# A hybrid decoder block: two of the six value jobs computed together as seven block products

## The chip, the cores and the metric

The kernel runs on one core of a Trainium2 chip. The metric is the device time in microseconds of one execution, as the median of several runs; a separate profiled execution shows where the time lies. The engines are named as in the profile: PE (TensorE, the products), DVE (VectorE), ACT (ScalarE), POOL (GpSimd) and SP (which issues most of the transfers). Each executes its own instructions strictly in the order in which the program holds them, and waits where an instruction needs what another engine has not finished.

## What is computed

One layer on 1024 tokens of 1024 features in float32: a norm, one wide projection to queries, keys, values, convolution input and two gates, dilated attention in three groups of eight heads, a causal depthwise convolution with a layer norm, the gated sum of both, an output product, and a SwiGLU feed-forward part.

```python
h = rms_norm(x, g_pre_mix[l])
z = h @ w_in[l]
q, k, v, glu_in, z_ga, z_gc = jnp.split(
    z, np.cumsum([ATTN_W, ATTN_W, ATTN_W, 2 * CONV_CHANNELS, D_MODEL]).tolist(), axis=-1)
y_attn = dilated_attention_mixer(...)            # 3 groups x 8 heads of 64
u = lax.conv_general_dilated(u, ...) + b_dw      # 31 taps, 1024 channels
u = jax.nn.silu(layer_norm(u, g_ln, b_ln))       # the convolution's norm, over channels
merged = jax.nn.sigmoid(z_ga) * y_attn + jax.nn.sigmoid(z_gc) * y_conv
x = x + rms_norm(merged @ w_mix_out[l], g_post_mix[l])
```

The values `v` are 1536 columns: six jobs of 256 columns, one for each group (three) and half of its heads (two).

## The kernel before

Every float32 operand of a product is kept as a high part, rounded by ACT, and a low part, the difference, so that a product is three products: high by high, high by low, low by high. Most of the projection is computed by a scheme with seven block products in place of eight (`winograd`, `prod`): the weights are cut into A11, A12, A21, A22 and combined to S1 to S4, the tokens into B11, B21, B22 and combined to T1 to T4 (`block_sums`, kept in `B.T`), and three accumulators X, Z, V collect the seven products. There the weights are the stationary operand and 512 columns of tokens move.

The six value jobs (`v`, L1115 on) are done the plain way: a 128 by 128 block of tokens is stationary, the weights move. For each of 8 token tiles and 8 feature tiles there is a pair of products: L1139 with 512 columns (high tokens by high and low weights) and L1140 with 256 (low tokens by high weights), 64 pairs for a job. ACT copies the result from PSUM (L1150), POOL adds its two halves (L1161), and SP stores it to `d_v`. Weight parts come from `value_weights` (ACT L207, DVE L208).

The order is written out by hand. `tick()` is called after every few products; it runs the steps that `later(n, step)` has put down for n ticks ahead, the next piece of weight preparation, and the next step of every generator in the background. In a value job a tick is four products. Beside the value jobs runs `conv_norm` (L1486 on), one such generator: it loads the eight channel blocks of the convolution, takes the mean over channels by a product on PE (L1503), subtracts it (DVE L1512), squares (ACT L1515), adds the squares up (DVE L1518), has PE sum them over partitions (L469 in `rstd`), takes one over the root on ACT and DVE (L473 to L478), spreads that over partitions by transposes on PE (L484), multiplies (DVE L1530) and applies SiLU (ACT L1533). It works on whole blocks of 128 x 1024, in steps of three or four ticks.

The attention (`attention`) is a second generator; `beat()` runs its steps between the products. Its first score waits, in the program's order, until the norm is done (`normed` reaches 9) and the first values are stored (`vn`). Before a pair's scores, `double` sets up its keys on POOL: a memset (L1078) and two copies (L1079, L1080) for each head and each half of the tokens. For the first pair the first half is queued 17 ticks after `attention` begins, the second half within its second score step. Attention needs 96 score tiles; it begins in the third value job and ends among the products of the convolution's output (`unit`, L336 to L338), where `conv_split` also prepares operands on ACT and DVE.

The last of the query and key pairs (`qk_pair`) comes right before the value jobs; on its way out DVE finishes the convolution (L868 to L881) and POOL adds its last block to the channel sum `csum` (L893).

## Time and profile before

| | us |
|---|---|
| median of 3 runs | 1675.94 |
| lowest and highest run | 1675.64, 1676.26 |
| the profiled execution | 1676.75 |
| its span on the chip | 1675.0 |
| PE busy in it | 1658.9 |

The span is what the trace covers; the profiled execution's own time is 1.75 us more. A busy PE is not a PE at its peak: a product is counted busy from its start to its end, and products overlap, so the pitch from one start to the next is the better measure of what one costs. A row of the timeline gives the start in microseconds from the span's start, the length, the engine, the line, and the tile written and read; in brackets stands the idle time of the engine before it and what ended that. A group with "x2" is several instructions in a row.

### The profile page before, as it was taken

The page shows a single profiled execution, that of the slowest core. Times are in us where ns is not written, and L with a number is a line of the kernel's source. Part 1 is how long each engine was busy: PE and PEld are TensorE (multiplying, and loading weights), DVE is VectorE, ACT ScalarE, POOL GpSimd, SP SyncE. Part 2 cuts the span into 40 slices and gives each one's busy share as a digit, 9 for nine tenths or more (in the row PEclk, how much of TensorE's full clock was granted, in tenths as well). Part 3 has the DMA queues.
Part 4 walks back from the last instruction along what each step waited for, and adds up shares of the span by engine and source line. Part 5 has one row for each costly group of instructions (what it writes and reads, how often), then busy time and mean ns, then how long its engine had stood idle before and what let it go on. Part 6 is the DMA issues. An engine that isn't in the chain of part 4 may idle for free.

```text
span 1675.0 us, 23388 instructions
## 1 busy us (share of the span) xinstructions
PE 1658.9 (99%) x8027; PEld 1384.6 (83%) x8027; DVE 1272.3 (76%) x2268; ACT 828.3 (49%) x1646; POOL 542.5 (32%) x456
## 2 busy tenths in 40 slices
PE   9999999999999999999999999999999999999998
PEld 7787888888888889988788888888888888888886
DVE  7998987789899768778876746877655566576686
ACT  7454443443444588888713357633333333354453
POOL 0038777787876366877300300000000000000000
PEclk9999999999999999999999999999999999999999
DMA  4435433455566987879998524134232223494334
GB/s 182 153 102 187 143 132 126 153 176 192 177 176 161 286 273 224 257 220 286 297 272 310 176 88 171 56 132 151 84 118 94 95 95 119 165 375 120 115 119 157
DMA packets 165178, 289.64 MB, mean 173 GB/s; under 512 B 47689, under 2 KB 79812, under 8 KB 165060
## 3 DMA queue, kind: packets, MB, share of 16 engines
q1 hardware_dynamic: 164420, 287.45, 52.5%
q8 instruction: 63, 1.03, 0.3%
q14 instruction: 55, 0.45, 0.1%
q10 hardware_dynamic: 288, 0.52, 0.1%
q0 software_dynamic: 352, 0.18, 0.1%
HBM read 197.39 MB, written 95.42 MB: 175 GB/s over the span
## 4 chain that ended last, share of the span: by engine, by line
PE 87%; issue 5%; DVE 2%; POOL 2%; ACT 2%; DMA 1%; SPq 0%; DVEq 0%; ACTq 0%; POOLq 0%
PE p L354 16%; PE p L353 16%; PE p L352 16%; PE p L2282 13%; PE p L2026 5%; PE p L1139 5%; PE p L336 2%; PE p L337 2%; PE p L338 2%; PE p L1140 2%; PE p L655 2%; PE p L1339 2%; PE p L1305 1%; PE p L1266 1%; PE p L1262 1%
## 5 line engine op out<-in xcount | busy, mean ns | idle before, releaser
L352 PE MATMUL p<-b,b 128*128 128x512 f32 x1316 | 512.7, 390 | 0.1
L354 PE MATMUL p<-b,b 128*128 128x512 f32 x1316 | 512.4, 389 | 0.2
L353 PE MATMUL p<-b,b 128*128 128x512 f32 x1316 | 512.2, 389 | 0.1
L352 PEld LDWEIGHTS p<-b,b 128*128 128x128 f32 x1316 | 247.1, 188 | 52.7 <-ACT c L411 0.5
L354 PEld LDWEIGHTS p<-b,b 128*128 128x128 f32 x1316 | 247.1, 188 | 52.5 <-POOL b L215 1.5
L353 PEld LDWEIGHTS p<-b,b 128*128 128x128 f32 x1316 | 247.1, 188 | 51.7 <-DVE b L1477 0.5
L2282 PE MATMUL p<-b,b 128*128 128x512 f32 x924 | 209.6, 389 | 0.0
L2282 PEld LDWEIGHTS p<-b,b 128*128 128x128 f32 x924 | 173.5, 188 | 36.0
L868 DVE SCALAR_TENSOR_TENSOR p<-b,par,p 128x511 f32<-128x511 f32 (+14 forms) x232 | 163.6, 738 | 0.0
L1139 PE MATMUL p<-b,b 128*128 128x512 f32 x384 | 144.2, 408 | 0.1
L214 ACT CAST b<-d 128x1024 fp32r<-128x1024 f32 x82 | 86.1, 1050 | 100.7 <-POOL d L237 56.6
L215 POOL TENSOR_TENSOR b<-d,b 128x1024 fp32r<-128x1024 f32 x43 | 104.2, 2422 | 47.6 <-ACT b L214 39.0
L1477 DVE TENSOR_TENSOR b<-b,b 128x512 fp32r<-128x512 f32 x141 | 98.9, 708 | 16.0 <-ACT b L1476 14.4
L215 DVE TENSOR_TENSOR b<-d,b 128x1024 fp32r<-128x1024 f32 x39 | 47.6, 1221 | 79.3 <-ACT b L214 79.3
L1140 PE MATMUL p<-b,b 128*128 128x256 f32 x384 | 107.7, 280 | 0.0
L1476 ACT CAST b<-b 128x512 fp32r<-128x512 f32 x141 | 86.4, 619 | 40.9 <-PE p L2282 18.5
L336 PE MATMUL p<-b,b 128*128 128x512 f32 x240 | 96.3, 401 | 0.0
L214 ACT CAST b<-b 128x1024 fp32r<-128x1024 f32 x51 | 53.6, 1052 | 85.0 <-POOL b L246 38.7
L1280 ACT ACTIVATE c<-c,stat 128x128 f32<-128x128 f32 (+1 forms) x192 | 85.2, 447 | 18.2 <-DVE stat L1270 16.9
L337 PE MATMUL p<-b,b 128*128 128x512 f32 x240 | 93.6, 390 | 0.0
L338 PE MATMUL p<-b,b 128*128 128x512 f32 x240 | 93.6, 390 | 0.0
L2026 PE MATMUL p<-b,b 128*128 128x512 f32 x384 | 89.9, 392 | 0.0
(248 smaller groups left out, 2897.0 us busy)
## 6 DMA issues: line engine op xcount, KB each, us to landing
b<-w_in SPq DMA_DIRECT2D x33, 512.0 KB, 5.8
b<-w_fi SPq DMA_DIRECT2D x29, 512.0 KB, 4.4
d<-w_in SPq DMA_DIRECT2D x25, 512.0 KB, 4.2
dk<-c SPq DMA_DIRECT2D x48, 256.0 KB, 4.3
dq<-c SPq DMA_DIRECT2D x48, 256.0 KB, 3.6
b<-dk SPq DMA_DIRECT2D x48, 256.0 KB, 6.2
d<-w_fi SPq DMA_DIRECT2D x22, 512.0 KB, 3.5
dqS<-c SPq DMA_DIRECT2D x44, 256.0 KB, 2.1
```

The source lines that it names most:

```text
L214: self.nc.scalar.copy(hi, x)
L215: self.wsplit.tensor_tensor(lo, x, f(hi), op=OP.subtract)
L336: nc.tensor.matmul(ps, hi[:, s], a, start=kt == 0, stop=False)
L337: nc.tensor.matmul(ps, hi[:, s], b, start=False, stop=False)
L352: nc.tensor.matmul(ps, hi[:, s], a, start=first and kt == 0, stop=False, skip_group_check=True)
L353: nc.tensor.matmul(ps, hi[:, s], b, start=False, stop=False, skip_group_check=True)
L354: nc.tensor.matmul(ps, lo[:, s], a, start=False, stop=kt == 3, skip_group_check=True)
L868: nc.vector.scalar_tensor_tensor(A[i][:, j:], src[i][:, :H - j], w[i], A[i][:, j:], op0=OP.mult, op1=OP.add)
L1139: nc.tensor.matmul(ps, a, w, start=kt == 0, stop=kt == KT - 1, skip_group_check=True)
L1140: nc.tensor.matmul(ps[:, 256:], b, w[:, :256], start=False, stop=kt == KT - 1, skip_group_check=True)
L2026: nc.tensor.matmul(banks[tt][nh], st, wt[:, nh * H:(nh + 1) * H], start=bool(kt == 0 and a), stop=bool(kt == KT - 1 and b))
L2282: nc.tensor.matmul(acc[t], x, y, start=first and e == 0, stop=last and e == 2, skip_group_check=True)
```

## The change

The first two value jobs, group 0 and group 1 of the first half of the heads, become one task, `quad`. It is the scheme with seven block products: rows of A are the two jobs (256 columns each), columns of A the two halves of the 1024 features, and B is the tokens' `B.T` that the earlier pairs used, which therefore stays alive a little longer. The tokens' blocks are stationary and 256 columns of weights move, high or low. `quad_prod` is one block product: 4 feature tiles by 4 token tiles by 3, 48 products, with a tick after every sixth. The sums of the weights (`quad_sum`) are made on DVE, the high parts on ACT and the low parts on POOL (`quad_split`), at ticks given by hand; those of the first block product and the loads hang on the last query and key pair (`pair`). The results go from PSUM through ACT copies and DVE additions to `d_v` in smaller stores. The other four value jobs stay as they are.

`conv_norm` now works by token halves: 16 half blocks of 128 x 512 are loaded, reduced and scaled, one step every second tick, the two halves one after the other, with a column sum on PE and a `rstd` for each half. The means are taken at tick 7, the column sums at ticks 29 and 49 of the quad's 56. While it runs beside the quad it uses the same PSUM pool.

`attention` is begun at tick 43 of the quad, and the first pair's keys are set up in four pieces 17, 19, 21 and 23 ticks later, second half included.

```diff
+        elif n < len(J) and J[n][2] == "values":
+            self.quad_first(self.quads[0], (2, 9, 3, 4, 19, 28, 29, 30))
...
-        ps = self.bank("s")
+        tag = "s" if "s" in self.tags else "g"
+        ps = self.bank(tag)
...
+    def quad_load(self, q, k):
+        x = q["r"][k] = self.slot() if k < 2 else self.ring()
+        self.nc.sync.dma_start(x, q["src"][k])
+    def quad_sum(self, q, name):
+        r, add = q["r"], self.nc.vector.tensor_tensor
+        if name == "S1":
+            q["s"] = self.ring()
+            add(q["s"], r[2], r[3], op=OP.add)
+        elif name == "S3":
+            add(r[2], r[0], r[2], op=OP.add)
+        elif name == "S2":
+            add(r[0], r[0], q["s"], op=OP.add)
+        else:
+            add(r[1], r[0], r[1], op=OP.add)
+    def quad_split(self, q, name):
+        nc, r = self.nc, q["r"]
+        k = ("A11", "A12", "S1", "A22", "S2", "S4", "S3").index(name)
+        if k == 2:
+            x, q["s"] = q["s"], None
+        else:
+            x = r[(0, 1, None, 3, 0, 1, 2)[k]]
+        hi, lo = self.slot(F32R), self.slot(F32R)
+        nc.scalar.copy(hi, x)
+        if k > 2:
+            r[(3, 0, 1, 2)[k - 3]] = None
+        nc.gpsimd.tensor_tensor(lo, x, f(hi), op=OP.subtract)
+        q["w"][name] = hi, lo
+    def quad_first(self, q, t):
+        for k, step in zip(t, [lambda: self.quad_load(q, 0), lambda: self.quad_load(q, 1), lambda: self.quad_load(q, 2),
+                               lambda: self.quad_load(q, 3), lambda: self.quad_split(q, "A11"),
+                               lambda: self.quad_sum(q, "S1"), lambda: self.quad_sum(q, "S3"),
+                               lambda: self.quad_sum(q, "S2")]):
+            self.later(k, step)
+    def quad_prod(self, ps, w, rhs, first):
+        nc = self.nc
+        hi, lo = w
+        for kt in range(4):
+            a, b = rhs[kt]
+            n = slice(kt * 256, (kt + 1) * 256)
+            for c in range(4):
+                o = ps[c // 2][:, c % 2 * 256:(c % 2 + 1) * 256]
+                t = slice(c * 128, (c + 1) * 128)
+                nc.tensor.matmul(o, a[:, t], hi[:, n], start=first and kt == 0 and c % 2 == 0, stop=False,
+                                 skip_group_check=True)
+                nc.tensor.matmul(o, a[:, t], lo[:, n], start=False, stop=False, skip_group_check=True)
+                nc.tensor.matmul(o, b[:, t], hi[:, n], start=False, stop=kt == 3 and c % 2 == 1, skip_group_check=True)
+                if c % 2:
+                    self.tick()
+    def quad(self, q, T, then):
+        nc, w = self.nc, q["w"]
+        last = then is None
...
...
+        def copy(ps, job, small=False):
+            x = result(small)
+            for b in range(2):
+                d = ordered(x[b], job[0][0])
+                if job is ja:
+                    nc.scalar.copy(d, plain(ps[b]))
+                else:
+                    nc.scalar.activation(d, plain(ps[b]), AF.Identity, scale=-1.0)
+            return x
+        def add(ps, x, job, hf):
+            for b in range(2):
+                d = ordered(x[b], job[0][0])
+                if job is ja:
+                    nc.vector.tensor_tensor(d, plain(ps[b]), d, op=OP.add)
+                else:
+                    nc.vector.tensor_tensor(d, d, plain(ps[b]), op=OP.subtract)
+            self.later(4, lambda: store(x, job, hf))
+        def two():
+            return [self.bank(), self.bank()]
+        ja, jb = q["jobs"]
+        for k, step in ((1, lambda: self.quad_split(q, "A12")), (5, lambda: self.quad_sum(q, "S4")),
+                        (9, lambda: self.quad_split(q, "S2")),
+                        (17, lambda: self.quad_split(q, "S1")), (25, lambda: self.quad_split(q, "S3")),
+                        (33, lambda: self.quad_split(q, "S4")), (41, lambda: self.quad_split(q, "A22"))):
+            self.later(k, step)
+        X, Z = two(), two()
+        self.quad_prod(X, w.pop("A11"), operands("B11"), True)
+        x1 = copy(X, ja, True)
+        self.quad_prod(Z, w.pop("A12"), operands("B21"), True)
+        add(Z, x1, ja, 0)
+        Z = x1 = None
+        self.quad_prod(X, w.pop("S2"), operands("T2"), False)
+        x2 = copy(X, ja)
+        V = two()
+        self.quad_prod(V, w.pop("S1"), operands("T1"), True)
+        v1 = copy(V, jb)
+        self.quad_prod(X, w.pop("S3"), operands("T3"), False)
+        add(X, v1, jb, 1)
+        v1 = None
+        self.quad_prod(V, w.pop("S4"), operands("B22"), False)
+        add(V, x2, ja, 1)
+        V = x2 = None
+        self.quad_prod(X, w.pop("A22"), operands("T4"), False)
+        o = result()
+        for b in range(2):
+            nc.scalar.activation(ordered(o[b], jb[0][0]), plain(X[b]), AF.Identity, scale=-1.0)
+        def end():
+            store(o, jb, 0)
+            self.vn = jb[1] + 1
+        self.later(3, end)
...
-        self.later(17, lambda p=nxt: self.double(p, 0))
+        for i in range(4):
+            self.later(17 + 2 * i, lambda p=nxt, i=i: self.double(p, i // 2, (i % 2,)))
...
-                if u == 1:
-                    self.double(cur, 1, (1,) if cur[2]["z"][1] else (0, 1))
+                if u == 1 and s:
+                    self.double(cur, 1, (1,))
...
+        add = nc.vector.tensor_tensor
+        A = {}
+        def load(hf, j):
+            x = self.slot()
+            for e in range(2):
+                b = 2 * j + e
+                nc.sync.dma_start(x[:, e * H:(e + 1) * H], self.d_conv[b][:, hf * H:(hf + 1) * H])
+                A[hf, b] = x[:, e * H:(e + 1) * H]
+        def average(hf):
+            ps = self.bank()
+            nc.tensor.matmul(ps, self.mean_col.to_broadcast([128, 128]), self.csum[:, hf * H:(hf + 1) * H],
+                             start=True, stop=True)
+            m = self.half()
+            nc.scalar.copy(m, ps)
+            return m
+        for j in range(4):
+            self.later((1, 3, 8, 11)[j], lambda j=j: load(0, j))
+        yield 5
+        means = [average(0), average(1)]
         self.csum = None
         yield 1
...
+        scale = [None, None]
         for hf in range(2):
...
+            mean, means[hf] = means[hf], None
+            q = []
+            for b in range(10):
+                if b < 8:
+                    add(A[hf, b], A[hf, b], mean, op=OP.subtract)
+                if 0 < b < 9:
+                    q.append(self.half())
+                    nc.scalar.activation(q[-1], A[hf, b - 1], AF.Square)
+                if b > 2:
+                    p = q.pop(0)
+                    add(q[0], q[0], p, op=OP.add)
+                p = None
+                if hf == 0 and b > 5:
+                    load(1, b - 6)
+                yield 1
+            mean = None
+            scale[hf] = self.rstd(q[0], H, self.eps_ln, 0)
+            next(scale[hf])
+            q = None
+        for hf in range(2):
+            yield 0 if hf == 0 else 2
+            try:
+                next(scale[hf])
+            except StopIteration as e:
+                pb = e.value
+            rs = self.half()
+            nc.scalar.copy(rs, pb[0])
+            pb = None
+            for b in range(9):
+                if b < 8:
+                    add(A[hf, b], A[hf, b], rs, op=OP.mult)
+                if b:
+                    a = A.pop((hf, b - 1))
+                    nc.scalar.activation(a, a, AF.Silu, bias=self.col(C_BLN + b - 1), scale=self.col(C_GLN + b - 1))
+                    self.later(4, lambda b=b, a=a, hf=hf: nc.sync.dma_start(self.d_act[b - 1][:, hf * H:(hf + 1) * H], a))
+                    a = None
+                    if hf:
+                        self.normed = b
+                yield b % 2
+            if hf:
+                nc.scalar.activation(rs[:, :1], self.eps_ln, AF.Exp)
+            rs = None
+        yield 2
...
+    vall = [(g, hg) for hg in range(2) for g in range(3)]
+    B.quads = [dict(jobs=[(vall[i + e], i + e) for e in range(2)], r=[None] * 4, w={},
+                    src=[aps["w_v"][2 * g + hg, c] for g, hg in vall[i:i + 2] for c in range(2)])
+               for i in range(0, 2 * QUADS, 2)]
     vj = {(g, hg): (job(aps["w_v"][2 * g + hg, 0], kind="values"), job(aps["w_v"][2 * g + hg, 1], kind="second"))
-          for hg in range(2) for g in range(3)}
+          for g, hg in vall[2 * QUADS:]}
...
-    B.banks(g=2, s=2, t=2, o=2)
-    B.bank("s")
     B.OT, B.merges = {}, []
     cn = B.bg(B.conv_norm())
     att = B.attention()
+    vs = list(vj.values()) + [late[:1] or co[:1]]
+    for i, q in enumerate(B.quads):
+        if i == QUADS - 1:
+            B.later(33, lambda: B.load_ahead(vs[0][0]))
+            B.later(43, lambda: next(att))
+            B.later(36, lambda: B.load_ahead(vs[0][1]))
+            B.later(41, lambda: B.queue_split(vs[0][1]))
+        B.quad(q, B.T, B.quads[i + 1] if i + 1 < QUADS else None)
+    B.T = None
+    B.banks(g=2, s=2, t=2, o=2)
+    B.bank("s")
     B.vsum = B.slot()
-    vs = list(vj.values()) + [late[:1] or co[:1]]
+    B.fine = att
     for i, (g, hg) in enumerate(vj):
-        B.v(g, hg, vs[i], vs[i + 1])
-        if i == 0:
-            next(att)
-            B.fine = att
-        elif i == 4:
+        if i == len(vj) - 1:
             assert cn not in B.gens
             cs = []
             B.later(16, lambda: cs.append(B.bg(B.conv_split())))
+        B.v(g, hg, vs[i], vs[i + 1])
     B.vsum = None
     B.RATE = RU
```

On POOL, from the end of the last query and key pair on. Before, the channel sum (L893) is followed by the value jobs' additions (L1161) and the first pair's keys (L1078 to L1080):

```order
L893 TENSOR_TENSOR b_1635<-b_1635,b_4834 128x1024
L1161 TENSOR_TENSOR d_4945<-b_4879 128x2x256 x2
L1161 TENSOR_TENSOR d_5051<-b_4879 128x2x256 x2
L1161 TENSOR_TENSOR d_5167<-b_4879 128x512 x2
L1078 MEMSET b_5233 64x512
L1079 CAST b_5233<-b_5108 64x512
L1080 CAST b_5114<-b_5106 64x512
```

Now (L898 is the channel sum, L1083 to L1085 the keys):

```order
L1199 TENSOR_TENSOR b_4819<-b_4726,b_4818 128x1024
L898 TENSOR_TENSOR b_1635<-b_1635,b_4836 128x1024
L1199 TENSOR_TENSOR b_4886<-b_4769,b_4885 128x1024
L1199 TENSOR_TENSOR b_4963<-b_4726,b_4962 128x1024
L1199 TENSOR_TENSOR b_5034<-d_4861,b_5033 128x1024
L1199 TENSOR_TENSOR b_5117<-d_4732,b_5116 128x1024
L1199 TENSOR_TENSOR b_5201<-b_4769,b_5200 128x1024
L1199 TENSOR_TENSOR b_5272<-d_4738,b_5271 128x1024
L1083 MEMSET b_5483 64x512
```

The low parts, each of 128 x 1024, stand where additions of 128 x 512 stood: that of A11 before the channel sum, those of A12, S2, S1, S3, S4 and A22 behind it. All four sets of the first pair's keys follow (the first of them begins with the last row).

On DVE, in the last third of the norm's subtractions and sums of squares, up to the reciprocal behind the column sums. Before:

```order
L1512 TENSOR_TENSOR b_4979<-b_4979,b_4887 128x1024
L1518 TENSOR_TENSOR b_5059<-b_5059,b_5032 128x1024
L1512 TENSOR_TENSOR b_5006<-b_5006,b_4887 128x1024
L1518 TENSOR_TENSOR b_5078<-b_5078,b_5059 128x1024
L1518 TENSOR_TENSOR b_5100<-b_5100,b_5078 128x1024
L1518 TENSOR_TENSOR b_5134<-b_5134,b_5100 128x1024
L474 RECIPROCAL rs_5208<-st_5207 128x8
```

Now, in the second half (L1671 subtracts, L1677 adds squares, L1274 takes a result of the quad from PSUM, L210 is a weight part of the next value job):

```order
L1671 TENSOR_TENSOR b_5123<-b_5123,c_4943 128x512
L1677 TENSOR_TENSOR c_5238<-c_5238,c_5220 128x512
L1274 TENSOR_TENSOR b_5189<-b_5189,p_4872 128x512
L1274 TENSOR_TENSOR b_5189<-b_5189,p_4873 128x512
L1671 TENSOR_TENSOR b_5139<-b_5139,c_4943 128x512
L1677 TENSOR_TENSOR c_5254<-c_5254,c_5238 128x512
L1671 TENSOR_TENSOR b_5139<-b_5139,c_4943 128x512
L1677 TENSOR_TENSOR c_5276<-c_5276,c_5254 128x512
L210 TENSOR_TENSOR b_5321<-b_5198,b_5321 128x2x256
L1677 TENSOR_TENSOR c_5308<-c_5308,c_5276 128x512
L1677 TENSOR_TENSOR c_5330<-c_5330,c_5308 128x512
```

The additions of the quad stand between the halves' steps, and the column sums wait for the last row, c_5330.

On PE, around the column sums of the first half, which stand inside the fourth block product (S1 by T1):

```order
L1221 MATMUL p_5108<-b_5033,b_915 128x256
L474 MATMUL p_5154<-mean_col,c_5120 128x1 x4
L1218 MATMUL p_5109<-b_5033,b_915 128x256
L1220 MATMUL p_5109<-b_5034,b_915 128x256
L1221 MATMUL p_5109<-b_5033,b_915 128x256
```

Before, eight such sums stood once, between products of the second value job:

```order
L1140 MATMUL p_5187<-b_5020,b_662 128x256
L469 MATMUL p_5198<-mean_col,b_5134 128x1 x8
L1139 MATMUL p_5187<-b_5047,b_672 128x512
L1140 MATMUL p_5187<-b_5047,b_672 128x256
L1139 MATMUL p_5187<-b_5047,b_695 128x512
```

They have become two groups of four, the first behind 174 and the second behind 294 of the quad's 336 products.

## Rows read from the trace of the kernel before

**Rows 1.** Busy time of each engine, and weight loads, from the page.

```profile
span 1675.0 us, 23388 instructions
PE 1658.9 (99%) x8027; PEld 1384.6 (83%) x8027; DVE 1272.3 (76%) x2268; ACT 828.3 (49%) x1646; POOL 542.5 (32%) x456
...
L352 PEld LDWEIGHTS p<-b,b 128*128 128x128 f32 x1316 | 247.1, 188 | 52.7 <-ACT c L411 0.5
```

**Rows 2.** Busy microseconds of each engine in stretches of the span.

```profile
560.00:575.00 15.00, 15.00 (x87) 13.02 (x86) 14.90 (x13) 9.02 (x13) 3.45 (x3) 1.00 0.91 299
...
770.00:830.00 60.00, 57.13 (x368) 48.29 (x366) 55.60 (x176) 51.33 (x163) 30.39 (x40) 1.00 0.99 306
```

**Rows 3.** Timeline of TensorE in the first value job (start, length, line).

```profile
544.69 0.40 PE L1139 MATMUL p<-b,b 128*128 128x512 f32 x1
...
547.52 0.40 PE L1139 MATMUL p<-b,b 128*128 128x512 f32 x1
...
548.29 1.98 PE L1503 MATMUL p<-b,mean_col 128*128 128x512 f32 x4 [0.26 <-POOL b L893]
```

**Rows 4.** Timeline of TensorE, four 256-column products in a row.

```profile
632.10 0.40 PE L1262 MATMUL p<-b,b 128*128 128x256 f32 x2
632.34 0.40 PE L1266 MATMUL p<-b,b 128*128 128x256 f32 x2
632.58 0.40 PE L1139 MATMUL p<-b,b 128*128 128x512 f32 x1
```

**Rows 5.** Timeline of TensorE where the first attention pair starts.

```profile
611.38 0.31 PE L1262 MATMUL p<-b,b 128*128 128x256 f32 x1
612.96 0.39 PE L1262 MATMUL p<-b,b 128*128 128x256 f32 x1 [1.27 <-POOL b L1079]
...
613.63 0.39 PE L1266 MATMUL p<-b,b 128*128 128x256 f32 x1 [0.17 <-POOL b L1080]
```

**Rows 6.** Timelines of VectorE and GpSimd, two places where they meet.

```profile
374.08 2.81 DVE L1005 TENSOR_TENSOR c<-c,c 128x512 fp32r<-128x512 f32 x1
...
373.95 2.40 POOL L215 TENSOR_TENSOR b<-d,b 128x1024 fp32r<-128x1024 f32 x1
...
559.13 2.32 DVE L1518 TENSOR_TENSOR b<-b,b 128x1024 f32<-128x1024 f32 x1
...
558.80 1.57 POOL L1161 TENSOR_TENSOR d<-b 128x512 f32<-128x512 f32 x1 [4.36 <-ACT b L1150]
```

**Rows 7.** Timeline of VectorE, neighbours of 512 and of 1024 columns.

```profile
544.10 0.68 DVE L208 TENSOR_TENSOR b<-b,b 128x512 fp32r<-128x512 f32 x1
544.70 0.69 DVE L881 TENSOR_TENSOR b<-p,c 128x512 f32<-128x512 f32 x1
...
568.83 1.21 DVE L1512 TENSOR_TENSOR b<-b,b 128x1024 f32<-128x1024 f32 x1
569.96 1.21 DVE L1518 TENSOR_TENSOR b<-b,b 128x1024 f32<-128x1024 f32 x1
```

**Rows 8.** Timelines of VectorE and TensorE at the end of the convolution norm.

```profile
572.23 5.90 DVE L1518 TENSOR_TENSOR b<-b,b 128x1024 f32<-128x1024 f32 x3
...
579.08 1.84 PE L469 MATMUL p<-mean_col,b 128*128 128x1 f32 x16
...
581.26 0.20 DVE L474 RECIPROCAL rs<-st 128x8 f32<-128x8 f32 x1 [3.13 <-ACT st L473]
```

**Rows 9.** DMA issues from 540 to 575: size, median microseconds to landing.

```profile
b<-dconv SPq DMA_DIRECT2D x8, 512.0 KB, 6.0
...
dconv<-b SPq DMA_DIRECT2D x1, 512.0 KB, 5.3
```

**Rows 10.** Timelines of VectorE and TensorE where attention's output product starts.

```profile
890.04 1.23 DVE L215 TENSOR_TENSOR b<-b,b 128x1024 fp32r<-128x1024 f32 x1 [0.66 <-ACT b L214]
...
901.02 0.39 PE L336 MATMUL p<-b,b 128*128 128x512 f32 x1
901.25 0.39 PE L337 MATMUL p<-b,b 128*128 128x512 f32 x1
```

75 lines of the change are left out of this document (27 added, 48 removed).

## The prediction

> **What bounds the kernel now.** I read the busy times first: PE is busy 1658.9 of the span's 1675.0 us [rows 1], so the change can only give back products or waits of PE, and can only cost by making PE wait. Then the table by stretches, for the stage that is touched [rows 2]: in the value stage from 560 to 575 us PE is busy all 15.00 us, and DVE 14.90 of them. Two engines are full there. PE makes the time, but DVE has nothing to spare, and the change hands DVE and POOL new work in just this stage. From 770 to 830, where attention lies among the convolution's output products, PE is idle 2.87 of 60 us and DVE busy 55.60. Then the timelines: of PE for the pitch of the products [rows 3, 4] and for its waits [rows 3, 5], of DVE and POOL for what happens where they meet [rows 6] and for the pitch of DVE's operations [rows 7], and the chain behind the norm's column sums [rows 8].
>
> **The products.** Removed are two jobs of 64 pairs. Between the two L1139 rows at 544.69 and 547.52 lie eight pairs [rows 3]: 2.83 / 8 = 0.354 us a pair, 128 pairs 45.3 us. Added are 7 x 48 = 336 products of 256 columns. A pair is 768 columns, so a third of it is 0.118; four products of 256 columns in a row, each with weights of its own, take from 632.10 to 632.58, 0.120 each [rows 4]. By the first 39.6 us, by the second 40.3. I take 39.6, since tokens and value weights are the operands there too. **Gain 5.7 us** (5.0 at the other end). The means (1.98 us) and the column sums (1.84 us, now twice 0.92) cost what they cost.
>
> **Two waits that go.** At the first attention pair PE is idle 1.27 and 0.17 us for the second half of its keys, which POOL copies only then [rows 5]. Now all four pieces are queued 17 to 23 ticks after tick 43, so about 17 ticks of 0.7 us before the first score, behind the last low part and beside two additions. **Gain 1.4** (0 if POOL is late). The means waited 0.26 for POOL's channel sum [rows 3]; they now come 42 products (5.0 us) into the stage instead of 20 products (3.6 us): **0.3**.
>
> **What the norm now asks of DVE and POOL.** Where both inputs of a DVE addition lie in SBUF, it and a POOL addition exclude each other. A DVE addition of 512 columns took 2.81 us when it came 0.13 us after a POOL subtraction of 2.40 us had begun: it got through only when that was done. One of 1024 columns took 2.32 us beside a POOL addition of 1.57, and 1.21 without one [rows 6, 7]. So in this stage their durations add. From the first product of the quad (t = 0) to the second group of column sums this is the list:
> - DVE, by pitch (0.60 us for 512 columns, 1.13 for 1024 [rows 7]): one low part of the last pair 0.6; the sums S3, S2, S4 3 x 1.13 = 3.4; 16 subtractions and 14 additions of halves 30 x 0.60 = 18.0; one weight part of the next value job 0.6. Together 22.6.
> - POOL: the channel sum and the low parts of A12, S2, S1, S3, S4, A22, seven of 2.40 less some 0.1 of overlap: 7 x 2.3 = 16.1.
>
> That is 38.7 us. They can begin when DVE has finished the convolution, about 1.5 us after t = 0 (the last convolution row on DVE is at 544.70, and behind it stand a sum of the quad, 1.13, in place of a weight part of 0.60, which also left earlier ticks). In the middle stand the first column sums, during which neither works: 0.92 us of PE, 0.34 from its end to the reciprocal (581.26 less 579.08 and 1.84), and five small operations, some 1.0 [rows 8]. So the second column sums can start at 1.5 + 38.7 + 2.3 = 42.5. PE without any wait is there after 294 products, the means and the first column sums: 294 x 0.118 + 1.98 + 0.92 = 37.6. The least that PE waits is 4.9.
>
> Four DVE operations that read PSUM (L1272, L1274, 2.4 us) come on top unless they lie beside POOL's. Going through the two queues in their order I find half of that hidden, 1.2 left, and some 0.3 for steps in which DVE waits for a square that stands on ACT behind a high part. **Waits of 6.4 us**, 4.9 to 8.5 as bounds (8.5: nothing hidden, and a turn lost at either group of sums). By that walk they fall in three places: about half a microsecond at the low part of A12, some 4 at the first column sums, whose last square stands on ACT behind the high part of S3 and whose last addition stands behind its low part, and some 2 at the second. What is queued behind the waiting column sums is every product of the quad, so all of it counts. Before, the same chain had the time: its 15 whole-block operations (17 us) were spread over 35 ticks, and the last ended at 578.13, a microsecond before the sums on PE began [rows 8].
>
> The Trainium skill, "SBUF — State Buffer", section "Who interferes with whom", has this as a rule: a DVE instruction with two inputs in SBUF and a GpSimd instruction that reads SBUF block each other for the whole instruction, whichever came first. The two places of rows 6 agree; what the Trainium skill adds there is that every one of the 30 halves is subject to it, so by it the waits are those above; if the halves could slip through beside POOL, DVE's own 22.6 + 2.4 + 1.5 + 2.3 = 28.8 us would be under PE's 37.6 and no wait would come.
>
> **Costed at nothing.** The quad's PSUM copies lie on ACT, busy 9.02 of 15 us [rows 2]; without that cover each would be late by its own half microsecond. Its weights are the same four loads of 512 KB, one pair earlier. SP issues 24 transfers more; nothing on PE waits for a store (the loads of the convolution are a rival below). The weight parts of the third job are made at ticks 44 to 56, ahead of their use.
>
> **The end of attention.** Its first score comes with 404 value products left instead of 432, 14 pairs or 5.0 us, and so its end moves 24 products further into the convolution's output, some 10 us of a stretch where PE idles 2.87 of 60 [rows 2]: **loss 0.5** (0 to 1). The merge behind it ended at 891.3, the first product that needs it began at 901.02, and the distance shrinks by 24 x 0.23 = 5.5 us [rows 10]; 4 us stay, so nothing waits.
>
> **The sum.** -5.7 - 1.4 - 0.3 + 6.4 + 0.5 = -0.5. The profiled execution took 1676.75 and would take 1676.2; the median of the runs is 0.8 lower, and from 1675.94 comes **1675.4**. With the ends: 4.9 us of waits and no loss behind give 1673.4, and half a microsecond less for a faster pitch 1673; 8.5 us, the slower pitch, attention's loss of 1 and a key wait that stays give 1680.
>
> **Rivals.** *A, the two queues fit.* DVE's steps reach the column sums in time, because POOL's low parts fall where DVE waits anyway or work ahead of the ticks is taken up. For it: before, PE never waited in a stretch with DVE busy 14.90 of 15 us. Against it: the list above is longer than PE's work. It decides at DVE and POOL together under 37.6 us. With 1 us of waits left: 1675.94 - 5.7 - 1.4 - 0.3 + 0.5 + 1.0 = 1670.0.
>
> *B, late blocks of the convolution; slower than before.* The eighth block is stored only after the stage has begun, behind four stores of the last pair on SP's queue, and its halves are loaded behind that store: 5.3 us for the store and up to 6.0 for a load [rows 9]. If the store goes out at 9 us, the half lands at about 20, and its subtraction is due at about 21. From 22 us on every microsecond goes into the first column sums; 4 us late gives 1675.4 + 4.1 = 1679.5. For it: the queue; against it: half-sized loads and fewer weights on the way.
>
> *C, weights that don't hide.* If the load of 128 columns of stationary tokens, 188 ns as recorded [rows 1], came between products of 256 columns, 336 x 0.188 = 63 us would be added, 1738. Rows 4 speak against it: 0.120 us with a load for each. The Trainium skill, "TensorE: Matmul & The Clock Gate", section "The mechanism", says that loads overlap running products only when their row groups differ, and by its figure for a load (section "LDWEIGHTS (loading the stationary operand)", columns / 1.2, 107 ns) an estimate is 36 us and 1711; the trace disagrees here.
>
> **How the numbers follow.** Forecast 0.62, A 0.24, B 0.12, C 0.02. The forecast's own range, 1673 to 1680, is nearly all within 0.2% (3.35 us, about what a measurement of this kernel can tell from no change: 1672.6 to 1679.3); 0.02 of it on either side. So faster 0.26, same 0.58, slower 0.16. For 8 in 10 the range takes in the forecast, most of A and the near end of B: 1669.5 to 1679.5.
>
> **What would show it.** The products: 256-column rows at a pitch of 0.118 to 0.120 in the quad. The waits: idle time of PE at L474, ended by DVE L1677, some 4 and some 2 us, with DVE halves of 0.69 us that take 2 to 3 us beside POOL's L1199. The keys: no wait for POOL's L1084 or L1085 at the first scores. B: a gap of DVE before L1671 that a DMA ends. I am wrong if PE passes both L474 groups without a wait (A), or if the waits lie at the low parts instead, which would mean that POOL and not DVE comes last.

## The result, and the profile after

The changed kernel takes 1682.24 us (median of 6 runs, 1679.74 to 1683.09), the kernel before 1675.79 (6 runs, 1675.25 to 1677.47): ratio 1.0035, interval 1.0022 to 1.0048. Run once more beside other kernels it took 1681.11 against 1675.62, 1.0032 (1.0020 to 1.0043). Forecast were 1675.4 us and no change; it is some 6 us slower, and outside the range of 1669.5 to 1679.5. Lines are those of the changed kernel, in which L1218 to L1221 are the quad's products, L474 the column sums, L1199 the low parts, L1671 and L1677 the norm's subtractions and additions, L1417 and L1421 the scores on TensorE and VectorE, L1464 the low parts of attention's weights.

The page of the changed kernel, span and busy times, answers to [rows 1]:

```profile
span 1679.8 us, 23634 instructions
PE 1658.0 (99%) x8107; PEld 1389.0 (83%) x8107; DVE 1284.2 (76%) x2298; ACT 829.7 (49%) x1654; POOL 550.8 (33%) x455
```

The profiled execution took 1681.56 us, 4.8 more than the profiled one of before. PE is no busier than before, though it has 5 us less to do and is idle more: its products take longer somewhere. The stretches of the quad show where (start and end, length, then busy time and instructions of PE, PEld, DVE, ACT and POOL, the granted clock, DMA share, GB/s):

```profile
560.00:567.90 7.90, 7.90 (x68) 7.90 (x67) 7.90 (x11) 4.22 (x8) 2.40 (x1) 1.00 0.60 191
567.90:572.00 4.10, 0.30 (x4) 0.10 (x2) 3.39 (x3) 2.81 (x4) 2.34 (x1) 1.00 0.90 285
572.00:577.00 5.00, 5.00 (x30) 5.00 (x31) 3.30 (x9) 1.66 (x4) 0.00 (x0) 0.66 0.42 161
```

PE stands for 4 us, and in the 5 us behind that the granted clock is 0.66 on average: part of it at 1.2 GHz, the rest at 2.4. PE's own timeline of the two groups of column sums (start, length, line, idle time before and what ended it):

```profile
567.78 0.28 PE L1220 MATMUL p<-b,b 128*128 128x256 f32 x1
567.90 0.28 PE L1221 MATMUL p<-b,b 128*128 128x256 f32 x1
571.98 1.05 PE L474 MATMUL p<-mean_col,c 128*128 128x1 f32 x8 [3.80 <-DVE c L1677]
572.89 0.46 PE L1218 MATMUL p<-b,b 128*128 128x256 f32 x1
573.14 0.42 PE L1220 MATMUL p<-b,b 128*128 128x256 f32 x1
573.36 0.42 PE L1221 MATMUL p<-b,b 128*128 128x256 f32 x1
...
576.35 0.32 PE L1220 MATMUL p<-b,b 128*128 128x256 f32 x1
576.51 0.28 PE L1221 MATMUL p<-b,b 128*128 128x256 f32 x1
...
588.73 0.28 PE L1221 MATMUL p<-b,b 128*128 128x256 f32 x1
590.55 1.05 PE L474 MATMUL p<-mean_col,c 128*128 128x1 f32 x8 [1.54 <-DVE c L1677]
591.47 0.36 PE L1218 MATMUL p<-b,b 128*128 128x256 f32 x1
591.67 0.28 PE L1220 MATMUL p<-b,b 128*128 128x256 f32 x1
```

The waits stand where they were forecast and nearly as long: from start to start, less the pitch, 3.96 and 1.70 us, both ended by the last addition on VectorE. New is what follows the first: from 573.14 to 576.35 the products come 0.214 us apart instead of 0.120, 15 such steps, **1.4 us**. Behind the second wait they keep their pitch. The cause of the waits, on VectorE and GpSimd:

```profile
555.19 4.70 DVE L1671 TENSOR_TENSOR b<-b,c 128x512 f32<-128x512 f32 x4
561.61 2.31 DVE L1671 TENSOR_TENSOR b<-b,c 128x512 f32<-128x512 f32 x1
...
567.46 1.46 DVE L1677 TENSOR_TENSOR c<-c,c 128x512 f32<-128x512 f32 x2
569.46 2.46 DVE L1677 TENSOR_TENSOR c<-c,c 128x512 f32<-128x512 f32 x1 [0.54 <-ACT c L1674]
...
574.39 2.49 DVE L1671 TENSOR_TENSOR b<-b,c 128x512 f32<-128x512 f32 x4
578.92 2.53 DVE L1677 TENSOR_TENSOR c<-c,c 128x512 f32<-128x512 f32 x1 [2.04 <-ACT c L1674]
...
555.17 2.96 POOL L1199 TENSOR_TENSOR b<-b,b 128x1024 fp32r<-128x1024 f32 x1 [2.30 <-ACT b L1196]
560.97 2.40 POOL L1199 TENSOR_TENSOR b<-d,b 128x1024 fp32r<-128x1024 f32 x1 [2.84 <-ACT b L1196]
569.03 2.34 POOL L1199 TENSOR_TENSOR b<-d,b 128x1024 fp32r<-128x1024 f32 x1 [5.66 <-ACT b L1196]
```

Four subtractions take 2.49 us without GpSimd and 4.70 with one of its low parts beside them; one addition takes 2.46 instead of 0.68. The last addition ahead of the first sums, at 569.46, is such a one. VectorE also waits for squares on ScalarE, 0.54 us there and 2.04 us at 578.92; the second of these squares stood behind two copies from PSUM and a high part.

At the first attention pair, [rows 5], the waits for the keys are gone, and another stands there (PE, ACT, DVE):

```profile
619.22 0.47 PE L1413 MATMUL p<-b,b 128*128 128x512 f32 x1 [1.15 <-DVE stat L1421]
...
615.92 1.28 ACT L1707 ACT_TABLE_LOAD   x1
617.22 0.20 ACT L1707 ACTIVATE c<-eps_ln 128x1 f32<-128x1 f32 x1
617.33 0.60 ACT L209 CAST b<-b 128x512 fp32r<-128x512 f32 x1
...
617.96 0.69 DVE L210 TENSOR_TENSOR b<-b,b 128x512 fp32r<-128x512 f32 x1 [2.91 <-ACT b L209]
618.57 0.28 DVE L1421 CUSTOM_DVE_ANT_0 c<-p,c 128x128 f32<-128x128 f32 x1
```

VectorE's scores stand behind the low part of a weight piece, whose high part stands on ScalarE behind the load of Exp's table. The change lets attention go 2 ticks after the norm's last step; before it was 11.

### The profile page after: what moved, and what is told of

Read it like the earlier page. It is cut to its first block, busy times and chain, and to the rows that moved or that the text cites. A ratio compares the mean times of both kernels' runs of the same rounds, so it can differ in the third digit from the quotient of the medians.

```text
span 1679.8 us, 23634 instructions
## 1 busy us (share of the span) xinstructions
PE 1658.0 (99%) x8107; PEld 1389.0 (83%) x8107; DVE 1284.2 (76%) x2298; ACT 829.7 (49%) x1654; POOL 550.8 (33%) x455
## 3 DMA queue, kind: packets, MB, share of 16 engines
q8 instruction: 64, 1.05, 0.3%
## 4 chain that ended last, share of the span: by engine, by line
PE 58%; DMA 3%; DVE 2%; ACT 2%; issue 1%; POOL 0%; DVEq 0%; SPq 0%; ACTq 0%; POOLq 0%
PE p L2460 12%; PE p L357 8%; PE p L358 8%; PE p L356 8%; PE p L2204 5%; PE p L1144 3%; PE p L340 2%; PE p L342 2%; PE p L341 2%; DMA b<-dk 2%; PE p L1490 2%; PE p L1145 1%; PE p L1456 1%; PE p L1417 1%; PE p L1413 1%
## 5 line engine op out<-in xcount | busy, mean ns | idle before, releaser
L356 PE MATMUL p<-b,b 128*128 128x512 f32 x1316 | 512.7, 390 | 0.0
L358 PE MATMUL p<-b,b 128*128 128x512 f32 x1316 | 512.4, 389 | 0.3
L357 PE MATMUL p<-b,b 128*128 128x512 f32 x1316 | 512.1, 389 | 0.1
L2460 PE MATMUL p<-b,b 128*128 128x512 f32 x924 | 209.6, 389 | 0.0
L1144 PE MATMUL p<-b,b 128*128 128x512 f32 x256 | 98.0, 410 | 0.3 <-DVE b L210 0.3
L340 PE MATMUL p<-b,b 128*128 128x512 f32 x240 | 96.6, 402 | 0.0
L341 PE MATMUL p<-b,b 128*128 128x512 f32 x240 | 93.8, 391 | 0.5 <-DVE b L1628 0.5
L342 PE MATMUL p<-b,b 128*128 128x512 f32 x240 | 93.7, 390 | 0.0
L2204 PE MATMUL p<-b,b 128*128 128x512 f32 x384 | 90.0, 392 | 0.0
L217 POOL TENSOR_TENSOR b<-b,b 128x1024 fp32r<-128x1024 f32 x24 | 57.7, 2405 | 86.5 <-ACT b L216 86.5
```

What stands on the lines that cost most here:

```text
L217: self.wsplit.tensor_tensor(lo, x, f(hi), op=OP.subtract)
L340: nc.tensor.matmul(ps, hi[:, s], a, start=kt == 0, stop=False)
L341: nc.tensor.matmul(ps, hi[:, s], b, start=False, stop=False)
L342: nc.tensor.matmul(ps, lo[:, s], a, start=False, stop=kt == nk - 1)
L356: nc.tensor.matmul(ps, hi[:, s], a, start=first and kt == 0, stop=False, skip_group_check=True)
L357: nc.tensor.matmul(ps, hi[:, s], b, start=False, stop=False, skip_group_check=True)
```

## Where TensorE loses, over all kernels

So that kernels can be compared by stage, each product's distance to the next start, less the median of that for its kind (line and shape, over all 18 profiles), is summed; I call it the excess. It counts waits and slow products alike. First the stage from the first value product to attention's first score, then attention beside the value products, then attention beside the convolution's output products; all in us of one profiled execution. "Slow" is what the products at half clock lose from the stage on; a number behind a plus sign is lost in attention, at some 806 us, and the 2.5 of "first sums late" in two places, at 590 and 620 us. The 0.6 of "DVE + both late" and the 1.4 of "before, keys, pause 2" lie in attention too. Column sums at half clock are not in it. The last columns are timed: medians, and the ratio to the kernel before with its interval.

| kernel | stage | att., values | att., conv. | slow | median / before | ratio |
|---|---|---|---|---|---|---|
| before | 0.9 | 3.7 | 7.1 | 0 | | |
| changed | 8.3 | 2.9 | 8.8 | 1.4 | 1682.2 / 1675.8 | 1.0035 (1.0022-1.0048) |
| changed, again | 9.3 | 3.6 | 8.1 | 1.6 | 1681.1 / 1675.6 | 1.0032 (1.0020-1.0043) |
| low parts on DVE | 6.0 | 3.4 | 8.5 | 1.6+0.9 | 1678.9 / 1676.7 | 1.0014 (1.0005-1.0024) |
| norm by halves alone | 7.0 | 5.2 | 6.4 | 1.9 | 1682.2 / 1676.7 | 1.0031 (1.0021-1.0042) |
| quad, old norm | 18.9 | 3.4 | 7.5 | 3.2 | 1692.3 / 1676.7 | 1.0095 (1.0080-1.0110) |
| first sums late | 7.4 | 4.9 | 8.3 | 2.5 | 1681.6 / 1676.7 | 1.0028 (1.0017-1.0038) |
| DVE + first late | 7.0 | 2.7 | 8.5 | 1.6+0.9 | 1678.7 / 1676.6 | 1.0018 (1.0009-1.0027) |
| ... + RV 0.45 | 5.7 | 5.0 | 6.5 | 0.7+0.9 | 1678.2 / 1676.6 | 1.0009 (1.0000-1.0018) |
| ... + pause 5 | 5.7 | 6.1 | 7.9 | 0.8 | 1683.5 / 1676.6 | 1.0050 (1.0035-1.0065) |
| keys alone | 0.4 | 2.6 | 7.3 | 0 | 1675.1 / 1676.6 | 0.9997 (0.9988-1.0006) |
| DVE + both late | 1.3 | 1.8 | 11.5 | 0.6 | 1674.6 / 1675.6 | 0.9992 (0.9983-1.0001) |
| ... + RV 0.45 | 1.6 | 4.0 | 8.5 | 0 | 1674.0 / 1675.6 | 0.9990 (0.9981-1.0000) |
| both late, POOL | 2.8 | 1.4 | 10.1 | 0 | 1676.6 / 1676.1 | 1.0000 (0.9990-1.0009) |
| before, att. later | 0.5 | 2.5 | 8.1 | 0 | 1676.7 / 1676.0 | 1.0004 (0.9995-1.0013) |
| before, keys, pause 2 | 0.3 | 9.2 | 7.4 | 1.4 | 1681.7 / 1676.0 | 1.0039 (1.0026-1.0053) |
| changed, pause 6 | 8.2 | 2.9 | 9.0 | 1.3 | 1680.7 / 1676.4 | 1.0029 (1.0018-1.0040) |
| DVE, both late, RV, pause 8 | 1.6 | 4.3 | 10.3 | 0 | 1676.8 / 1676.4 | 1.0003 (0.9994-1.0013) |

Ahead of the first value product the excess is 3.5 to 5.9 us, and that differs with the execution, not with the kernel: it is 4.9 in the first profile of the changed kernel and 3.6 in the second. Behind attention it is nil, but for 1.8 us in one kernel.

## Experiments: the waits at the column sums

**Low parts on VectorE.**

```diff
-        nc.gpsimd.tensor_tensor(lo, x, f(hi), op=OP.subtract)
+        nc.vector.tensor_tensor(lo, x, f(hi), op=OP.subtract)
```

> The changed kernel with the seven low parts of the quad (L1199) on VectorE instead of GpSimd. Theory 1 (the additions of VectorE and the subtractions of GpSimd exclude each other, their sum is what the column sums wait for, and the wait then drops TensorE's clock): seven operations of 1024 columns add 7 x 1.13 = 7.9 us to VectorE's list and take 16.1 us of GpSimd's out of the sum, so the list falls from 42.5 to about 34.5 us against 37.6 of TensorE. TensorE waits under 1 us at both L474 groups (now 4.0 and 1.7), no product of the quad after the first sums runs at 0.213 us, and the time falls by about 6 to 7 us, to 1675 to 1677. Theory 2 (the squares on ScalarE, which stand behind the high parts, are what comes last, wherever the low parts run): the waits at L474 stay at 3 us or more in all and the time is 1680 to 1683.

2.2 us over the kernel before, where the changed kernel is 5.5 to 6.4 over it. The waits at the sums fall to 1.77 and 1.45 us, 3.2 together instead of 5.7: taking GpSimd away helps as theory 1 says, but not down to under 1 us each. VectorE loses turns that I had not counted, and here theory 2 has its share: it waits 0.80 and 2.41 us for high parts on ScalarE.

```profile
565.84 1.23 DVE L1199 TENSOR_TENSOR b<-d,b 128x1024 fp32r<-128x1024 f32 x1 [0.80 <-ACT b L1196]
...
574.61 1.23 DVE L1199 TENSOR_TENSOR b<-b,b 128x1024 fp32r<-128x1024 f32 x1 [2.41 <-ACT b L1196]
...
568.50 1.05 PE L474 MATMUL p<-mean_col,c 128*128 128x1 f32 x8 [1.61 <-DVE c L1677]
```

And the clock fell again, behind the wait of 1.77 us (the last row; 1.61 us of it PE is idle). Neither theory had that, and the time is above the forecast 1675 to 1677.

**First sums late.** The first `next(scale[0])` moves behind the seventh subtraction of the second half:

```diff
+                if hf and b == 6:
+                    next(scale[0])
...
-            next(scale[hf])
+            if hf:
+                next(scale[1])
```

> The changed kernel with the first half's column sums moved into the second half's loop, behind its seventh subtraction; nothing else moves. Theory 1 (the sum of the two engines' work counts, not the place): no wait at the first sums and VectorE loses no 2 us around them, but the second sums then wait some 3 us instead of 1.8, since the list is still longer than TensorE's products: 1677 to 1680, the lower if the clock stays at its high level. Theory 2 (each wait belongs to its place): the first wait and the slow products behind it go, the second stays at 1.8 us: 1675.5 to 1677.

The mechanism of theory 1, though 1681.6 us is hardly under the changed kernel. No wait at the first sums, but 3.27 at the second, and 1.16 and 0.40 at products whose low part is late. The waits are owed to the list, not to a place.

**Both edits.**

> The changed kernel with both edits: the seven low parts of the quad on VectorE, and the first half's column sums behind the seventh subtraction of the second half. Theory 1 (what is lost is the wait at the first sums and the clock that falls behind it): the wait of 1.8 us and the 1.6 us of slow products that the kernel with the low parts on VectorE alone still had both go, the second wait stays at 1.5 us or less: 1678.9 - 3.4 = 1675.5, from 1674.5 to 1676.5. Theory 2 (the clock falls behind any group of column sums that TensorE waits for): the fall moves to the second sums, and 1677 to 1678 is left.

A miss: 1678.7, no better than the low parts alone. PE goes past the first sums, then waits 2.87 us at the second, about the 3.2 that it waited before in two parts, and the clock falls there instead. PE's timeline of this kernel, at its one wait:

```profile
582.03 0.28 PE L1221 MATMUL p<-b,b 128*128 128x256 f32 x1
585.02 1.87 PE L474 MATMUL p<-mean_col,c 128*128 128x1 f32 x8 [2.71 <-DVE c L1677]
586.75 0.56 PE L1218 MATMUL p<-b,b 128*128 128x256 f32 x1
587.11 0.41 PE L1220 MATMUL p<-b,b 128*128 128x256 f32 x1
```

**Second sums later too.** Four more ticks ahead of the second half's `rstd`:

```diff
             if hf:
+                yield 4
                 next(scale[1])
```

> The kernel with the low parts on VectorE and the first sums late, with the second column sums 4 more ticks (2.8 us of products) behind the last addition's turn. Theory 1 (VectorE's list alone is still some 3 us longer than TensorE's products up to the second sums, and the clock falls because of that wait): the wait of 2.9 us shrinks to 0.2 us, the 1.6 us of slow products behind it go, attention begins 4 ticks later and gives back up to 1 us: 1678.7 - 2.7 - 1.6 + 0.5 = 1674.9, from 1674 to 1676.5. Theory 2 (the wait moves on with the sums, since other work comes in on VectorE): a wait of 2 us or more stays, 1677.5 to 1679.

Theory 1: 1674.6, which is 1.0 under the kernel before (interval -2.8 to +0.2) instead of 2.1 over it, and 3.7 us less by the two profiles (3.8 were worked out). The same place in the timelines of PE and VectorE:

```profile
585.65 0.28 PE L1221 MATMUL p<-b,b 128*128 128x256 f32 x1
585.77 0.95 PE L474 MATMUL p<-mean_col,c 128*128 128x1 f32 x8
586.58 0.36 PE L1218 MATMUL p<-b,b 128*128 128x256 f32 x1
586.78 0.28 PE L1220 MATMUL p<-b,b 128*128 128x256 f32 x1
...
583.49 1.48 DVE L1677 TENSOR_TENSOR c<-c,c 128x512 f32<-128x512 f32 x2
```

VectorE's last addition ends at 584.97; in the kernel with two edits PE's wait for it ended at 585.02, and both stages began within 0.01 us of each other. The list is as long as ever, and PE now has products to do meanwhile. The wait goes, and with it the fall of the clock behind it (one that costs 0.6 us is left in attention): the excess in the stage is 1.3 instead of 7.0, while attention, which starts later against its products, gives back 2.

**The same with the low parts back on GpSimd.**

> The kernel with both groups of column sums later, but with the seven low parts on GpSimd as the change has them. Theory 1 (the subtractions on GpSimd cost VectorE their own length, whatever the sums wait for): the waits at the sums are under 1 us, but TensorE now waits 1 to 2 us at products whose low part (L1199) is late, and the clock mostly stays: 1676 to 1678, that is 1.5 to 3 us over the kernel with the low parts on VectorE. Theory 2 (with the sums late nothing is due any more that GpSimd could hold up): within 0.7 us of that kernel, 1674 to 1675.3.

Theory 1, at its lower end: 0.4 over the kernel before instead of 1.0 under it. The intervals of the two overlap, so the times alone don't show the difference; the profiles do, with an excess in the stage of 2.8 instead of 1.3, and this row on PE (1.16 us from start to start, and 0.40 once more):

```profile
572.24 0.39 PE L1220 MATMUL p<-b,b 128*128 128x256 f32 x1 [1.00 <-POOL b L1199]
...
576.47 2.52 DVE L1677 TENSOR_TENSOR c<-c,c 128x512 f32<-128x512 f32 x1 [1.33 <-ACT c L1674]
...
576.04 2.41 POOL L1199 TENSOR_TENSOR b<-b,b 128x1024 fp32r<-128x1024 f32 x1 [3.85 <-ACT b L1196]
```

Wherever the sums stand, an addition of 0.68 us takes 2.52 beside a low part of 2.41. The Trainium skill, "SBUF — State Buffer", section "Who interferes with whom", says that a VectorE instruction with two inputs in SBUF contends with a GpSimd instruction that reads SBUF, and that the ports they share are locked exclusively; the trace agrees.

**The norm by halves alone, and the quad with the old norm.** The first puts the new `conv_norm`, with its pause of 2 ticks before attention, into the kernel before, the second the old one, with 11, into the changed kernel; the PSUM tiles come from the pool that is there:

```diff
-            ps = self.bank()
+            ps = self.bank("s")
...
-            ps = self.bank("s")
+            ps = self.bank()
```

> The kernel before with the convolution's norm by token halves alone: no block products, keys as before. Theory 1 (the halves cost only together with GpSimd's low parts of the quad): GpSimd has only the channel sum and some copies of 1.3 us here, so each column sum waits 0 to 2 us; 1676 to 1678.5. Theory 2 (the norm by halves is dear by itself, since its two chains are denser than the whole-block chain): waits at both sums as in the changed kernel, 1680 to 1682.

> The changed kernel with the old whole-block norm (its PSUM tiles from the quad's pool) beside the quad. Theory 1 (sum of VectorE and GpSimd): at the one group of column sums, due some 26 us into the stage, VectorE has 1.5 + 17 + 3.4 + 0.6 us and GpSimd five operations of 2.3 us ahead of it, 34 us: one wait of 6 to 8 us, the clock falls behind it, and the time is 1679 to 1683, no better than the changed kernel. Theory 2 (the halves are the cause): a wait of 2 us at most, 1674 to 1677.

Both have causes of their own. With halves alone PE is idle 3.78 us at the first sums and the clock falls; the time, 1682.2, is about that of theory 2, but by luck, since there VectorE had waited for the convolution's halves, which come late behind the stores of the last pair. That is my rival B, in another kernel:

```profile
560.92 0.69 DVE L1520 TENSOR_TENSOR b<-b,c 128x512 f32<-128x512 f32 x1 [3.23 <-DMA b<-dconv]
561.53 0.69 DVE L1526 TENSOR_TENSOR c<-c,c 128x512 f32<-128x512 f32 x1
563.29 0.69 DVE L1520 TENSOR_TENSOR b<-b,c 128x512 f32<-128x512 f32 x1 [1.08 <-DMA b<-dconv]
...
570.52 1.87 PE L469 MATMUL p<-mean_col,c 128*128 128x1 f32 x8 [3.78 <-DVE c L1526]
```

With the old norm beside the quad PE waits 6.57 us for a low part, not at the sums: GpSimd itself had waited for a buffer that a store of the convolution was still reading; at 1692.3 us the time is outside both forecasts. Neither tells the theories apart.

```profile
565.48 2.34 POOL L1199 TENSOR_TENSOR b<-b,b 128x1024 fp32r<-128x1024 f32 x1 [12.36 <-DMA dconv<-b]
```

**The changed kernel again**, without an edit.

> The changed kernel once more, for a second profile of it and for times beside the others of this call. Theory 1 (the 1.2 us that it lost ahead of 45 us in its profile come and go between executions of any of these kernels, and the fall of the clock behind the first column sums comes in every one): TensorE's excess ahead of 45 us lies anywhere from 1.4 to 3.5 us, the slow products behind the first sums are there again with 1.2 to 1.8 us; 1680 to 1683. Theory 2 (both are of that one execution or of this kernel alone): no slow products, or the start late by the same 1.2 us.

Theory 1: 1.44 us ahead of 45 us instead of 2.82, slow products of 1.59 us again, 1681.1. This time the clock fell before the sums began, and they are slow too, 1.87 us instead of 1.05, so that the fall cost 2.4 us:

```profile
570.62 1.87 PE L474 MATMUL p<-mean_col,c 128*128 128x1 f32 x8 [3.79 <-DVE c L1677]
```

## Experiments: attention

**The keys alone**, in the kernel before.

```diff
-        self.later(17, lambda p=nxt: self.double(p, 0))
+        for i in range(4):
+            self.later(17 + 2 * i, lambda p=nxt, i=i: self.double(p, i // 2, (i % 2,)))
...
-                if u == 1:
+                if u == 1 and s:
```

> The kernel before with the sooner copies of the first pair's keys alone. Theory 1 (as forecast: the 1.27 and 0.17 us are all that is lost at the first pair, and the wait for VectorE's scores that stands there in the changed kernel comes from the norm's shorter pause before attention): 1.0 to 1.5 us under the kernel before. Theory 2 (the scores on VectorE come last as soon as the keys do not): no more than 0.5 us under it.

1.5 us under the kernel before by the medians (interval -2.0 to +1.0), and no wait for a key: theory 1 as far as the times can tell; by the profile the excess from the first value product on falls from 11.7 to 10.2.

**The place of attention's end.** `yield 11` to `yield 18` in the kernel before:

> The kernel before, with the pause between the norm's last step and attention 18 instead of 11 ticks: attention starts 14 pairs later, with 404 value products left as in the changed kernel, and nothing else differs. Theory 1 (the forecast's term: the end of attention lies 24 products further on in the convolution's output, priced by PE's idle time there): +0.5 us, 0 to 1. Theory 2 (every attention step that moves from the value products to the convolution's output costs more there, as the 1.0 and 1.75 us of the two profiles of the changed kernel say): +1 to +2.5 us.

0.7 us slower (interval -0.8 to +2.2). Beside the value products the excess falls by 1.2, beside the convolution's it rises by 1.0. The forecast's 0.5 fits; the interval reaches into theory 2's 1 to 2.5 as well, but the profile, with 0.2 less in all, gives that no support.

**The rate**, `RV, RU = 0.45, 0.8` in the kernel with both edits, and then in the one with both sums later:

> The kernel with both edits, and RV, the rate at which attention's steps go out beside the value products, 0.45 instead of 0.42, so that 404 value products carry as many steps as 432 did before and attention ends at the same place of the convolution's output. Theory 1 (the 1.9 us that TensorE idles more from 780 to 845 us come from attention's end lying 24 products further on): they go, and 0.5 to 1 us comes back as waits in the denser stretch: 1.0 to 1.9 us under the kernel with both edits. Theory 2 (they come from how attention's own steps meet the weight parts, wherever it ends): within 0.7 us of that kernel, or slower.

> The kernel with the second sums later and RV 0.45, so that attention ends where it did in the kernel before. Theory 1 (what the end wins, the denser stretch gives back, as with RV 0.45 before): within 0.8 us of the kernel with the second sums later. Theory 2 (the end alone counts): 1 to 2 us under it.

Both are 0.5 us under the kernel without the edit; of the first I had expected 1.0 to 1.9. What the end wins (2.0 and 3.0 us of excess) the value stretch gives back (2.3 and 2.2). The last of them, 1674.0 us, is the fastest kernel here: 1.6 us under the kernel before, interval 0 to 3.2.

**The pause between norm and attention.** 2 instead of 11 ticks in the kernel before with the keys; 5, 6 and 8 instead of 2 in three of the others, all by one line:

```diff
-        yield 11
+        yield 2
         self.normed = 9
```

> The kernel before with the sooner key copies and a pause of 2 instead of 11 ticks between the norm and attention, as in the changed kernel; whole-block norm, no block products. Theory 1 (with so short a pause the first scores meet the last Silu, the load of Exp's table and the weight part behind them): a wait of 1 to 2 us for VectorE's scores stands at the first pair, which takes back the 1.4 us of the keys; attention ends 6 us sooner, which gives 0 to 1 us: 0 to 1 us slower than the keys alone. Theory 2 (the wait comes from the halves' multiplications, which are still queued): no wait above 0.6 us at the first scores, and 1.5 to 2.5 us under the kernel before.

> The kernel with both edits and RV 0.45, and attention is let go 5 instead of 2 ticks after the norm's last step (it was 11 before). Theory 1 (the wait of 1.2 to 1.8 us at the first scores is VectorE behind a weight part whose high part stands on ScalarE behind the last Silu and the 1.28 us load of Exp's table): the wait falls under 0.4 us, attention begins and ends 2 us later, and the time is 0.5 to 1.5 us under the kernel with RV 0.45. Theory 2 (VectorE's list as a whole is late there): the wait stays above 1 us and the time is the same or longer.

> The changed kernel with a pause of 6 instead of 2 ticks between the norm and attention, nothing else (11, as before, leaves no room for its buffers). Theory 1 (the short pause is what took the keys' gain back): the wait of 1.2 to 1.9 us at the first scores falls under 0.5 us, attention begins 2.8 us later, which by the kernel with attention moved alone costs 0.4 us: 0.5 to 1.5 us under the changed kernel, 1679.8 to 1681. Theory 2 (every other start only deals attention's later waits anew, as RV 0.45 with 5 ticks did): 2 us or more over the changed kernel, with the excess in attention and not at the first scores.

> The fastest kernel so far (low parts on VectorE, both sums later, RV 0.45) with a pause of 8 instead of 2 ticks. Theory 1: the 0.3 and 1.1 us that it waits at the first scores and behind them go, attention begins 4.2 us later, 0.6 us: 0.3 to 1 us under it, 1673 to 1674. Theory 2: attention's waits are dealt anew, 1675 to 1679.

In the kernel before the short pause is dear: 5.8 us over it, where the keys alone are 1.5 under; far more than theory 1 gave, and not by the wait that I had named. ScalarE's last Silu and the load of Exp's table hold the first exponentials until 605.04, and operands of a later score come late by DMA. PE's timeline:

```profile
609.87 0.90 PE L1340 MATMUL p<-c,b 128*128 128x256 f32 x4 [1.46 <-ACT c L1313]
...
618.99 0.30 PE L1267 MATMUL p<-b,b 128*128 128x128 f32 x1 [2.32 <-DMA c<-rep]
620.20 0.30 PE L1267 MATMUL p<-b,b 128*128 128x128 f32 x1 [0.91 <-DMA b<-dq]
```

In the changed kernel a pause of 6 takes the wait at the first scores away, 0.30 us is left, and yet nothing is won that the times can tell (1.0029 beside 1.0035 and 1.0032): from its first score to its last product attention takes 227.70 us, with the short pause 227.65. The stretches, of the kernel with a pause of 6 and of the changed kernel:

```profile
618.64:846.34 227.70, 219.17 (x1572) 197.17 (x1571) 187.67 (x624) 189.84 (x594) 151.62 (x207) 1.00 0.87 257
```

```profile
617.10:844.75 227.65, 220.98 (x1577) 198.24 (x1575) 186.27 (x625) 190.82 (x599) 150.77 (x207) 1.00 0.91 258
```

With 5 ticks the time rose by 5.3 us (by the medians), with 8 by 2 (by the ratios), where theory 1 had both fall. Attention's excess, both columns together, lies between 9.9 and 16.6 us over these kernels, with the same steps: every other start puts them beside other weight parts and loads. Why one start is dear and another is not stays open.

## Why the prediction was wrong, step by step

- **Products.** Some 310 pairs of neighbours in the quad without a wait lie 0.1198 us apart: 336 x 0.1198 = 40.3, a gain of 5.0. The 5.7 that I took was the better end of my two; -0.7.
- **The list of VectorE and GpSimd.** Right: waits of 3.96 and 1.70 and 0.2 at the low part of A12, 5.9 against 6.4, at the places named, from the cause named. Yet the list itself was 1.4 us longer than in my sum: the second sums began 45.4 us into the stage, not 44.0. VectorE's waits for squares, which I had at 0.3 us, were 0.54 and 2.04; the copies ahead of the second on ScalarE I had costed at nothing. PE without its waits was 1.9 later than in my sum as well, 1.4 of it for the next reason, 0.5 by the pitch. That the waits came out right is luck in part: the two errors cancel.
- **The clock, the first step that failed.** I priced a wait of PE at its length alone and what comes behind it at nothing. The first wait also left products at 0.214 us instead of 0.120 behind it: 1.4 and 1.6 us in the two profiles, 2.4 in the second with its column sums. In the timed runs the mean granted clock is 0.995 to 0.998, that of the kernel before 0.998 to 0.999.
- **Means.** The 0.26 us is gone, as forecast.
- **Attention's start, the second step that failed.** Forecast for attention was -1.4 for the keys and +0.5 for its end, together -0.9; its excess rose from 10.8 to 11.7, +0.9. The keys alone are worth the 1.4 by the profile. But the change also cuts the pause from 11 to 2 ticks, which stands in the diff and which I did not price. Both profiles show attention's excess at 11.7, the kernel before with the keys alone has 9.9: 1.8 us lost, where I had 0.5. The pause alone can cost that and more (some 7 us in the kernel before); in the changed kernel a longer one does not bring it back, so the cause of this part stays open.
- **Attention's end.** 0.5 (0 to 1) against 0.7 measured alone (interval -0.8 to +2.2): not contradicted, and not to be told from nothing.
- **Rivals.** A is refuted, the queues did not fit. B's mechanism showed in the norm alone, not in the changed kernel. C is refuted by the pitch.

The sum by the first profile: -5.0 + 5.9 + 1.4 - 0.3 + 0.9 for attention = +2.9; with 0.9 of difference ahead of the stage, 3.8 of the 4.8 us. Another 0.46 is a wait for a weight part (L210) at 599 us; the rest is in small pieces. The medians differ by more, 5.5 to 6.4: the profiled execution of the kernel before lies 1.0 us over its median, that of the changed kernel 0.7 under its own. Three of the changed kernel's six first runs have a mean clock of 0.995 or 0.996, where the profiled one has 0.998; what they lost by that is not shown, since no such run has a profile.

## What to carry to other kernels

Price a wait of TensorE with what comes behind it: look in the trace whether the products after a wait of that length keep their pitch. Where a chain on another engine is too long, moving its consumer to another place only moves the wait; give TensorE other work until the chain ends (here 4 ticks of products, which took 3 to 4 us off), and shorten the chain. A pause that looks like slack (`yield 11`) is a term of the sum as well: ask what it kept apart.

## What was not expected of the hardware

- Waits and the granted clock: behind nine waits of 1.77 to 3.96 us at the column sums 0.7 to 1.9 us were lost at 1.2 GHz in the products alone; behind those of 1.70, 1.69, 1.68 and 1.45 nothing. The length of a wait does not decide alone: at attention's first scores waits of 1.91 us (changed kernel again) and 1.87 (norm by halves) left the clock at its high level, and one of 2.40 (first sums late) did not. Before, 16 column sums in a row without a wait, 1.84 us, left the clock at its high level [rows 8].
- The mean clock goes with the time in some kernels: of the ten runs of the kernel with both sums later, those at 0.999 and 1.000 took 1672.98 to 1673.10 us, those at 0.998 1674.16 to 1674.64, those at 0.997 1675.06 to 1677.38. It is not all: with both edits, eight runs at 0.996 lie anywhere from 1678.21 to 1681.45.
- From the start to 45 us the same products lose 1.2 to 3.7 us, differently in each of the 18 profiles: in some the first products come at half clock for some 3 us longer. A difference of 1 us between two profiles says nothing before that is taken out.
